# Moving low parts to GpSimd and the list steps closer together at the front of the up stage of a two-layer encoder trunk

## The chip, the cores and the metric

One Trainium2 chip, of which the kernel uses one core. The time is the device time of one execution in microseconds, the median of several runs. The engines are TensorE (PE in the profile; PEld is its weight load), VectorE (DVE), ScalarE (ACT), GpSimd (POOL) and SyncE (SP), each with an instruction queue that it works off in order; transfers run on 16 DMA engines.

## The reference

The trunk has two layers on 256 tokens of width 1024: a latent attention and a sparse attention, each followed by an expert mixer (PEER). The change lies in the mixer, which both layers have. Its core:

```python
best, pos = lax.top_k(cand, PEER_TOPK)                     # per token and head: 16 of 16384 experts
expert = jnp.take_along_axis(cand_idx, pos, axis=-1)
gate = jax.nn.softmax(best, axis=-1)
...
u = w_down[e_blk]
a = jnp.einsum('td,ted->te', x_blk, u).astype(jnp.float32)
hg = (jax.nn.gelu(a, approximate=False) * g_blk).astype(w_up.dtype)
return jnp.einsum('te,ted->td', hg, w_up[e_blk]).astype(x_blk.dtype)
```

There are 8 heads with 16 experts each, so 128 experts per token, out of 128 x 128. Inputs and outputs are float32.

## The kernel before

**Staging.** A layer's mixer computes the queries and the scores, picks experts on VectorE and GpSimd, and then streams the expert tables through TensorE. The *down stage* multiplies all 128 blocks of 128 experts of `w_down` with the 256 tokens and leaves the gated activations in a large array `A` in SBUF (`arena` in the profile). The *up stage* multiplies activations with rows of `w_up` into four PSUM banks `y`. float32 products are made of two float16 parts, high and low: a product is high x high + high x low + low x high, three matmuls for one.

**The stream of weights.** `Stream` (lines 178 to 299) carries every weight block (128 x 1024, float32, 512 KB) from memory. `_load` (210) brings a block into one of six `raw` buffers: by SyncE for a whole block (222), by an indirect DMA of GpSimd for a *listed* one (219). `_high` (233) makes the high part on ScalarE (line 166), `_low` (240) the low part on VectorE (line 175), with a sum that a later check of the number range uses. High and low parts have rings of six. `get` (279) takes the next block and splits up to three blocks ahead and loads up to eight ahead. If `share` is n, every n-th block goes through `_pooled` (246) in `_split` (268): ScalarE scales the raw block in place (253) and rounds it to the high part (255), GpSimd subtracts (257), and four blocks later ScalarE makes the sum (266). Both layers use this in earlier stages, where `share` is 4 or 3; in the up stage it is 0.

**The up stage** (from 1623) has 118 blocks. The first 22 (`HEAD`) are dense: a block of 128 experts for both token tiles, twelve matmuls in `rows` (500). Then come 72 listed blocks with 24 further dense ones in between (two at a time). A listed block holds one expert row per partition, picked so that only experts that some token chose are fetched: 40 of them serve both token tiles, 32 serve one (six matmuls). `USES` holds the order, `PAIRS` and `FIRSTS` say which pairs of activations it needs and from which use on. `cut` (1536) splits a pair of activations into high (`xh`, ScalarE) and low (`xl`, VectorE).

**The lists.** Which rows a listed block holds comes from the chosen experts. `lists` (1398) is a generator of 24 steps, mostly on VectorE: taking the eight largest of a row and replacing them, again and again (1417, 1418), then ranks, one small TensorE product `base` (1441), four one-hot tiles `to` (1480), each with eight small matmuls that send entries to other partitions (`moved`, 1475), and at the end the row numbers `up_at` (1491) and `act_at` (1493, 1496). `list_on(n)` (1513) makes n steps. Two calls of `list_on(3)` come in the last blocks of the down stage, the rest in the head of the up stage.

**Stores and returns.** Activations that listed blocks need are first stored to memory: `store` (1501) issues one transfer of 256 KB on SyncE (1508). `gather` (1519) then returns them by row number, two or three indirect DMAs on GpSimd into a tile `V` or `U` (1527, 1532). The first three gathers are issued in the head, each later one three groups ahead of its use.

**What sets the order.** A planner orders the instructions of each engine, except where the code forces it. `pe` and `dve` (444, 447) put each instruction behind the one before it on TensorE and VectorE, as long as the chain has an entry in `chains`. Both chains are on from the down stage until they are dropped in the head (`chains.pop`). While they are on, rows, list matmuls, lows, activation splits and list steps run in the order in which they are written. ScalarE's, GpSimd's and SyncE's order is the planner's, but `gp` (453) puts a gather behind the last indirect load written ahead of it.

Of the kernel before, what the change touches and what calls it, by code (L numbers as in the profile page):

```python
# [68 lines left out]
DENSE, HEAD = 46, 22  # L69
# [260 lines left out]
def tile_trunk(ctx: ExitStack, tc: tile.TileContext, ins, out: bass.AP, short, shared):  # L330
# [17 lines left out]
    def oh_tile(tag, dt=F32):  # L348
        return ohp.tile([P, 4, P], dt, tag=tag, name=tag)
# [64 lines left out]
    ws = Stream(nc, raws, rings, half, split, spare16)  # L414
# [38 lines left out]
    def gp(emit):  # L453
        with ExitStack() as order:
            if ws.fetched is not None:
                order.enter_context(tc.issue_after(ws.fetched))
            return emit()
# [42 lines left out]
    def rows(o4, lhs, blk, start, stop, tiles=(0, 1)):  # L500

        h, l = blk
        lh, ll = lhs
        for t in tiles:
            tsl = slice(t * P, (t + 1) * P)
            todo = [(w, rr, i, n) for i, (w, rr) in enumerate(((lh, h), (lh, l), (ll, h))) for n in range(2)]
            if stop:
                todo.sort(key=lambda z: z[3])
            for w, rr, i, n in todo:
                ins = mm(o4[t][n], w[:, tsl], rr[:, n * 512 : (n + 1) * 512], start and i == 0, stop and i == 2)  # L510
        return ins
# [663 lines left out]
    def peer(li):  # L1175
# [325 lines left out]
        def store(half, upto):  # L1501

            b0 = stored[half]
            b1 = min(b0 + CHUNKED, NKEYS)
            if b0 < b1 <= upto:
                ts = slice(half * P, (half + 1) * P)
                rows_of = abuf[(b0 - DENSE) * P : (b1 - DENSE) * P, ts].rearrange("(b a) t -> a b t", a=P)
                nc.sync.dma_start(rows_of, A[:, b0:b1, ts])  # L1508
                stored[half] = b1
# [3 lines left out]
        def list_on(n):  # L1513
            for _ in range(n):
                next(listing[0], None)
# [3 lines left out]
        def gather(g):  # L1519
            if g >= len(GROUPS):  # L1520
                return
            t = oh_tile("VU"[g % 2])
            for slot, c in enumerate(GROUPS[g][:2]):
                at = act_at[:, c : c + 1]
                if c < BOTHS:
                    o = t[:, 2 * slot : 2 * slot + 2, :].rearrange("p a b -> p (a b)")
                    gp(lambda: nc.gpsimd.indirect_dma_start(o, None, abuf, bass.IndirectOffsetOnAxis(ap=at, axis=0)))  # L1527
                    continue
                halves = abuf.rearrange("e (h t) -> (e h) t", h=2)
                for h in range(2):  # L1530
                    at = act_at[:, c + h * JO : c + h * JO + 1]
                    gp(lambda: nc.gpsimd.indirect_dma_start(t[:, 2 + h, :], None, halves,  # L1532
                                                            bass.IndirectOffsetOnAxis(ap=at, axis=0)))
            gathered[g] = t

        def cut(n):
            if n >= len(PAIRS):
                return
            kind, k = PAIRS[n]
            if kind == "listed":  # L1540
                a = gathered.pop(k).rearrange("p (s h) t -> p s (h t)", s=2)
            else:
                a = A[:, k : k + 2, :]
            slot = slice(2 * n % NC, 2 * n % NC + 2)
            hh, al = xh[:, slot, :], xl[:, slot, :]
            total = split.total("most")
            act(lambda: split.high(hh, a, A_UNIT))
            dve(lambda: split.low(al, a, A_UNIT, hh, total))
            made[n] = [(hh[:, j, :], al[:, j, :]) for j in range(2)]
# [51 lines left out]
        def operand(k):  # L1601
            if k % 2 == 0 and k not in parts:
                a = A[:, k : k + 2, :]
                slot = slice(k % NC, k % NC + 2)
                hh, al = xh[:, slot, :], xl[:, slot, :]
                total = split.total("most")
                split.high(hh, a, A_UNIT)
                split.low(al, a, A_UNIT, hh, total)
                for j in range(2):
                    parts[k + j] = (hh[:, j, :], al[:, j, :])  # L1610
            return parts[k]
# [3 lines left out]
        def middle_loads():  # L1615
            held.append(load_x(lnar, keep))
            held.append(load_affine(lnar, li, 1))
            if last and short:
                least()
                split.seen = BOTH + split.n["most"]  # L1620
                weigh_up(0, 0, split.seen)

        if short:
            for i, (n, slot, tiles) in enumerate(USES):
                if i == FIRSTS[n]:
                    cut(n + 1)
                    if PAIRS[n][0] == "listed":
                        gather(PAIRS[n][1] + 3)
                if i < len(USES) - STAGGER:
                    rows(y4, made[n][slot], ws.get(), i == 0, False, tiles)  # L1630
                if i < HEAD - 9:
                    list_on(1)
                    store(0, NKEYS)
                    store(1, NKEYS)
                if i == HEAD - 9:
                    list_on(99)
                    while stored != [NKEYS, NKEYS]:
                        store(0, NKEYS)
                        store(1, NKEYS)
                    chains.pop("dve")  # L1640
                    chains.pop("pe")
                if HEAD - 9 <= i < HEAD and (HEAD - 1 - i) % 3 == 2:
                    gather((i - HEAD + 9) // 3)
                if i == len(USES) // 2:
                    middle_loads()
            items = [(made[n][slot], tiles) for n, slot, tiles in USES[-STAGGER:]]
        else:
            for k in range(NKEYS - STAGGER):
                rows(y4, operand(k), ws.get(), k == 0, False)
                if k == 64:  # L1650
                    middle_loads()
            items = [(operand(k), (0, 1)) for k in range(NKEYS - STAGGER, NKEYS)]
# [67 lines left out]

    mla()
    peer(0)
    dsa()
    return peer(1)


# [91 lines left out]
```

## Time and profile before

| | us |
|---|---|
| median of 3 runs (1676.13 to 1681.88) | 1680.58 |
| the profiled execution | 1678.09 |
| its span, first to last instruction | 1676.3 |
| granted TensorE clock | 0.992 |

A row of a timeline gives the start and the length in microseconds, the engine, the line, the operation, what it writes and reads, the number of instructions merged, and in brackets the idle time before it and what ended that. A row of groups gives the busy time and the mean in ns, then the idle time before. A row of waits says who waited for whom: total, times, longest. A line like L460 or L175 is a helper's, so the names of the tiles tell where an instruction belongs: `y` is the up stage, `d` the down stage, `raw<-in_up,up_at` a listed load, `V<-abuf` or `U<-abuf` a return, `lo` a low part of a weight block and `xl` one of an activation pair.

### The profile page before, as it was taken

The numbers are of one execution on the slowest core, as the hardware profiler recorded it, in microseconds if no ns is written. First come the engines' busy times: TensorE is split into PE (matmuls) and PEld (weight loads), VectorE is DVE, ScalarE is ACT, GpSimd is POOL, SyncE is SP. The second block draws the span as 40 slices with busy tenths as digits, with TensorE's granted clock in tenths as the row PEclk, the third lists the DMA queues.
The fourth block names the chain that finished last, engine by engine and source line by source line (L and its number), as shares of the span: only waits on it lengthen the run. The fifth ranks groups of instructions, "written<-read, shape, count | busy, mean of one in ns | idle before, by whom it ended". The sixth has DMA issues, their size and how long they took to land.

```text
span 1676.3 us, 33243 instructions
## 1 busy us (share of the span) xinstructions
PE 1609.7 (96%) x12451; PEld 1163.6 (69%) x12451; DVE 1347.5 (80%) x3212; ACT 1064.2 (63%) x1865; POOL 531.3 (32%) x419
## 2 busy tenths in 40 slices
PE   9999999999999999999899999999999999999995
PEld 7678888999996443444577688888999974444432
DVE  8689999989997756666788799999989978466565
ACT  7666656888884445554568665576888854455452
POOL 2011255000000277877032022441000000788783
PEclk9999999999999999999999999999999999999998
DMA  9445656655758677777855555556547567777773
GB/s 342 157 171 173 203 179 208 209 164 179 231 184 249 243 256 250 265 259 244 298 199 172 185 184 179 202 183 218 169 154 252 181 206 271 247 262 254 271 241 132
DMA packets 139963, 361.44 MB, mean 216 GB/s; under 512 B 13712, under 2 KB 56848, under 8 KB 139792
## 3 DMA queue, kind: packets, MB, share of 16 engines
q1 hardware_dynamic: 112880, 268.51, 47.8%
q0 software_dynamic: 26624, 90.20, 16.5%
q8 instruction: 99, 1.62, 0.4%
q14 instruction: 72, 0.59, 0.1%
q10 hardware_dynamic: 288, 0.52, 0.1%
HBM read 333.35 MB, written 25.82 MB: 214 GB/s over the span
## 4 chain that ended last, share of the span: by engine, by line
PE 51%; DMA 11%; issue 11%; POOL 11%; DVE 11%; ACT 3%; SPq 2%; POOLq 0%; DVEq 0%; ACTq 0%
PE d L460 34%; DMA raw<-in_up,up_at 7%; DVE lo L175 5%; POOL raw L219 5%; PE y L460 4%; PE G L460 3%; PE pq L460 2%; POOL U L1527 2%; POOL U L1532 2%; PE seen L460 2%; ACT hi L166 2%; SPq L1508 1%; DMA raw<-in_up 1%; POOL V L1532 1%; PE qw L460 1%
## 5 line engine op out<-in xcount | busy, mean ns | idle before, releaser
L175 DVE SCALAR_TENSOR_TENSOR lo<-raw,hi 128x1024 f16<-128x1024 f32 (+2 forms) x550 | 695.5, 1275 | 217.0 <-ACT hi L166 169.6
L166 ACT ACTIVATE hi<-raw 128x1024 f16<-128x1024 f32 (+2 forms) x550 | 570.0, 1050 | 384.9 <-DMA raw<-in_up,up_at 169.1
L460 PE MATMUL d<-xh,lo 128*128 128x256 f16 x2048 | 558.5, 273 | 0.9 <-DVE lo L175 0.9
L460 PE MATMUL d<-xh,hi 128*128 128x256 f16 x2048 | 558.6, 273 | 0.0
L460 PE MATMUL d<-xl,hi 128*128 128x256 f16 x2048 | 558.5, 273 | 0.0
L460 PEld LDWEIGHTS <-hi 128*128 128x128 f16 x5016 | 489.0, 98 | 57.7 <-issue 0.9
L219 POOL DMA_INDIRECT raw<-in_up,up_at x144 | 172.1, 1195 | 612.4 <-DVE act_at L1496 566.0
L460 PEld LDWEIGHTS <-xh 128*128 128x128 f16 x1904 | 185.4, 98 | 251.2 <-issue 32.0
L460 PE MATMUL y<-lo,xh 128*128 128x512 f16 x880 | 265.2, 379 | 12.0 <-DVE lo L175 8.1
L460 PE MATMUL y<-hi,xh 128*128 128x512 f16 x880 | 264.0, 380 | 11.3 <-ACT hi L166 5.8
L460 PEld LDWEIGHTS <-lo 128*128 128x128 f16 x2508 | 245.8, 98 | 31.9 <-DVE lo L175 2.7
L460 PE MATMUL y<-hi,xl 128*128 128x512 f16 x880 | 264.4, 380 | 2.1 <-DVE xl L175 1.9
L1375 ACT ACTIVATE gate<-hot,rest 128x128 f16<-128x128 f16 x512 | 168.0, 406 | 20.6 <-DVE hot L1369 18.7
L460 PEld LDWEIGHTS <-xl 128*128 128x128 f16 x952 | 92.1, 98 | 120.9 <-DVE xl L175 7.5
L257 POOL TENSOR_TENSOR lo<-raw,hi 128x1024 f16<-128x1024 f32 x27 | 63.3, 2346 | 212.1 <-ACT hi L255 161.1
L1369 DVE TENSOR_TENSOR hot<-iota,place 128x1024 f16<-128x1024 f16 x128 | 87.7, 689 | 19.3 <-PE G L460 18.6
L460 PE MATMUL G<-gate,hot 128*128 128x128 f16 x1024 | 96.2, 219 | 2.1 <-DVE gate L1371 2.1
L460 PEld LDWEIGHTS <-hot 128*128 128x128 f16 x1536 | 92.8, 113 | 3.1 <-DVE gate L1371 2.4
L1290 POOL TENSOR_TENSOR arena<-arena 128x800 f32<-128x800 f16 x32 | 70.7, 2210 | 62.7 <-DVE arena L1287 62.7
L460 PE MATMUL seen<-gate,hot 128*128 128x128 f16 x512 | 89.1, 219 | 0.0
L1371 DVE TENSOR_TENSOR gate<-hot,gate 128x512 f16<-128x512 f16 x128 | 87.6, 687 | 0.0
L253 ACT ACTIVATE raw<-raw 128x1024 f32<-128x1024 f32 x27 | 28.6, 1057 | 88.7 <-DMA raw<-in_down 80.1
(270 smaller groups left out, 1828.2 us busy)
## 6 DMA issues: line engine op xcount, KB each, us to landing
raw<-in_down SPq DMA_DIRECT2D x256, 512.0 KB
raw<-in_up SPq DMA_DIRECT2D x92, 512.0 KB
abuf<-arena SPq DMA_DIRECT2D x80, 256.0 KB
raw<-in_peer_q SPq DMA_DIRECT2D x24, 512.0 KB
raw<-in_dsa_qk SPq DMA_DIRECT2D x16, 512.0 KB
raw<-in_mla_w_o SPq DMA_DIRECT2D x8, 512.0 KB
arena<-in_peer_q SPq DMA_DIRECT2D x8, 512.0 KB
raw<-in_dsa_v SPq DMA_DIRECT2D x8, 512.0 KB
```

The costliest lines, as they stand in the source:

```text
L166: return nc.scalar.copy(o, src) if unit == 1.0 else nc.scalar.mul(o, src, unit)
L175: return nc.vector.scalar_tensor_tensor(o, src, unit, hi, op0=ALU.mult, op1=ALU.subtract, accum_out=total)
L219: self.fetched = self.nc.gpsimd.indirect_dma_start(t, None, table, bass.IndirectOffsetOnAxis(ap=at, axis=0)).ins
L253: self.act(lambda: nc.scalar.mul(raw, raw, unit))
L257: nc.gpsimd.tensor_tensor(lo, raw, hi if short else hi.bitcast(F32), op=ALU.subtract)
L460: return pe(lambda: nc.tensor.matmul(o, l, r, start=start, stop=stop, skip_group_check=True))
L1290: nc.gpsimd.tensor_tensor(o.rearrange("p k c -> p c k"), same, cell[t][:, h, :, None].to_broadcast([P, CELLS, TOPK]), op=ALU.mult)
L1369: nc.vector.tensor_tensor(hot, iota4[:, None].to_broadcast([P, 2, P, 4]), place16[:, :, None, four].to_broadcast([P, 2, P, 4]), op=ALU.is_ ...
L1371: engine.tensor_tensor(gate[:, 0], hot[:, 1].rearrange("p c j -> p j c"), gate16[:, four, None].to_broadcast([P, 4, P]), op=ALU.mult)
L1375: nc.scalar.mul(gate[:, 1, j, :], hot[:, 1, :, j], rest[:, t : t + 1])
L1527: gp(lambda: nc.gpsimd.indirect_dma_start(o, None, abuf, bass.IndirectOffsetOnAxis(ap=at, axis=0)))
L1532: gp(lambda: nc.gpsimd.indirect_dma_start(t[:, 2 + h, :], None, halves, bass.IndirectOffsetOnAxis(ap=at, axis=0)))
```

## The change

```diff
         if short:
+            ws.share = 3
             for i, (n, slot, tiles) in enumerate(USES):
...
-                if i < HEAD - 9:
-                    list_on(1)
+                if i < HEAD - 12:
+                    list_on(2 if i < 8 else 1)
                     store(0, NKEYS)
                     store(1, NKEYS)
-                if i == HEAD - 9:
+                if i == HEAD - 12:
+                    ws.share = 0
                     list_on(99)
...
-                if HEAD - 9 <= i < HEAD and (HEAD - 1 - i) % 3 == 2:
-                    gather((i - HEAD + 9) // 3)
+                if HEAD - 12 <= i < HEAD - 9:
+                    gather(i - HEAD + 12)
```

`share` is 3 from the start of the up stage until block 10 has been taken. `get` splits three blocks ahead, so this concerns blocks 3 to 13 of the head; by their running numbers in the stream (block 0 is number 167 in the first layer, 466 in the second) blocks 5, 8 and 11 of the first layer and 3, 6, 9 and 12 of the second go through `_pooled`. Two list steps stand behind each of blocks 0 to 7 and one behind blocks 8 and 9, where one stood behind each of blocks 0 to 12 and the rest behind 13. The remaining stores, the end of the lists and the end of both chains stand behind block 10 instead of 13. The first three gathers stand behind blocks 10, 11 and 12 instead of 13, 16 and 19.

## The prediction

> **What bounds the kernel now.** I read the page first (busy shares, the 40 slices), then the busy time of each engine in three stretches: the first layer's up stage up to its first listed block, and both layers' from there to the last block.
>
> ```profile
> PE 1609.7 (96%) x12451; PEld 1163.6 (69%) x12451; DVE 1347.5 (80%) x3212; ACT 1064.2 (63%) x1865; POOL 531.3 (32%) x419
> POOL 2011255000000277877032022441000000788783
> ```
>
> Busy time by stretch (columns: length, then PE, PEld, DVE, ACT and POOL busy with counts, granted clock, DMA share, GB/s):
>
> ```profile
> 523.80:587.71 63.91, 58.65 (x299) 26.48 (x297) 48.49 (x124) 26.48 (x32) 9.44 (x9) 1.00 0.79 278
> 587.71:808.61 220.90, 210.97 (x956) 93.55 (x957) 135.91 (x267) 115.95 (x134) 167.45 (x136) 0.99 0.77 260
> 1436.71:1657.39 220.68, 211.60 (x960) 93.12 (x960) 136.88 (x270) 114.64 (x133) 169.96 (x139) 1.00 0.75 249
> ```
>
> Over the whole span TensorE is busy 96%, so no change of this kind can win much; GpSimd has 32%, which looks like room. The slices correct that: it is idle for long and then near 0.8 twice, in the two listed phases. What TensorE needs there comes from its pace:
>
> ```profile
> 526.22 0.59 PE L460 MATMUL y<-hi,xh 128*128 128x512 f16 x2
> 526.65 0.59 PE L460 MATMUL y<-lo,xh 128*128 128x512 f16 x2
> ```
>
> Two matmuls per 0.431 us, so 2.59 us for a dense block of twelve and 1.29 for a listed one with one token tile. From the first listed block on, an up stage has 64 blocks of twelve and 32 of six, 960 matmuls: 206.9 us. The stretches take 220.9 and 220.7, so 14.0 and 13.8 us are lost in them. Next the waits in the first of them, and GpSimd's issues:
>
> ```profile
> ACT hi L166 <- DMA raw<-in_up,up_at: 76.2, 35, 6.2
> PE y L460 <- ACT hi L166: 3.9, 4, 1.6
> PE y L460 <- DVE lo L175: 3.8, 5, 0.9
> ```
>
> ```profile
> 575.83:798.61 222.78, 212.95 (x968) 94.52 (x966) 134.09 (x263) 114.23 (x132) 176.88 (x144) 0.99 0.76 253
> 1424.72:1647.56 222.84, 212.67 (x969) 94.00 (x967) 134.80 (x265) 114.27 (x133) 178.41 (x145) 1.00 0.77 253
> ```
>
> ```profile
> POOL raw L219 <- issue: 20.1, 66, 0.3
> POOL raw L219 <- DVE lo L175: 2.9, 2, 1.7
> ```
>
> TensorE waits for high and low parts, and those for the rows that GpSimd fetches. GpSimd issues 144 indirect DMAs per layer (72 rows of up, 72 returned activations) in 222.8 us, 1.547 each; nearly all its idle time is 0.3 us between two issues, and only 2.9 us are waits for a buffer. So in the listed phase GpSimd's queue is the bound: 222.8 against TensorE's 206.9. What sets its start:
>
> ```profile
> 575.83 1.24 POOL L219 DMA_INDIRECT raw<-in_up,up_at  x1 [283.11 <-DVE act_at L1496]
> 582.39 1.24 POOL L1532 DMA_INDIRECT V<-abuf,act_at  x1 [0.30 <-issue]
> 587.03 0.63 ACT L166 ACTIVATE xh<-V 128x512 f16<-128x512 f32 x1 [0.58 <-DMA V<-abuf,act_at]
> 587.71 0.61 PE L460 MATMUL y<-hi,xh 128*128 128x512 f16 x2 [2.34 <-ACT xh L166]
> 1436.71 0.60 PE L460 MATMUL y<-hi,xh 128*128 128x512 f16 x2 [2.16 <-ACT xh L166]
> ```
>
> It stood 283 us until VectorE had written the lists. The first return goes out behind fetches, and TensorE stands 2.34 and 2.16 us for it. Together a layer has 16.3 (second: 16.0) us that a GpSimd queue far enough ahead would give back.
>
> **Lists earlier.** Of the 24 list steps six are done in the down stage (two calls of `list_on(3)`). The other 18 stand now at blocks 0 to 12 with the last five behind block 13; then at 0 to 9. VectorE runs lows, return splits and list steps in the written order:
>
> ```profile
> 528.22:575.15 46.93, 44.94 (x237) 20.60 (x236) 42.88 (x111) 20.87 (x24) 0.00 (x0) 1.00 0.81 286
> ```
>
> ```profile
> 528.22 0.69 DVE L1569 TENSOR_TENSOR arena<-arena,d 128x512 f32<-128x512 f32 x1 [2.51 <-ACT d L1568]
> ```
>
> ```profile
> L175 DVE SCALAR_TENSOR_TENSOR lo<-raw,hi 128x1024 f16<-128x1024 f32 x19 | 23.0, 1222 | 3.4 <-ACT hi L166 3.4
> L175 DVE SCALAR_TENSOR_TENSOR xl<-arena,xh 128x512 f16<-128x512 f32 x10 | 6.9, 686 | 0.0
> L1480 DVE TENSOR_TENSOR to<-iota,at 128x1024 f16<-128x1024 f16 x4 | 4.7, 1221 | 0.0
> L1417 DVE MAX8 U<-V 128x8 f32<-128x128 f32 x4 | 1.2, 292 | 0.0
> L1418 DVE MATCH_REPLACE8 V<-U,V 128x128 f32<-128x128 f32 x4 | 1.1, 276 | 0.0
> ```
>
> From 528.22 to the lists' end it idles 3.4 us. 19 lows are 21.8 at 1.15 each (1.222 in the record, but neighbours overlap, as the four `to` show: 4.7 of busy, not 4 x 1.221), ten splits at 0.61 are 6.1, L1569 0.6; the lists are the other 15.0 of the 43.5. With the change only lows 3 to 12 and five splits stand ahead of the lists' end, and lows 5, 8 and 11 go to GpSimd: 7 x 1.15 + 3.0 + 0.6 + 15.0 = 26.7, so 554.9 if VectorE never waits. With what it waits for (next part) I take 560: 15 us earlier. The second layer gives lows 3, 6, 9 and 12 away.
>
> **What GpSimd makes of it.** The seven issues of the first three returns go out at once, 7 x 1.55 = 10.9 us, and the last lands 4.6 us after its issue (582.39 to 587.03): at 575.5, 12 us ahead of use. So 2.34 and 2.16 us are gone. A fetch is tied to buffers: fetch 30 takes raw buffer 24, free after low 24, whose place in the ring of six is free after block 18. That is blocks 19 to 29 ahead of use, nine of 2.59 and two of 1.29, less 2.3 for high and low: 23.6 us. Before:
>
> ```profile
> 597.58 1.41 POOL L219 DMA_INDIRECT raw<-in_up,up_at  x1 [0.31 <-issue]
> 607.54 0.59 PE L460 MATMUL y<-hi,xh 128*128 128x512 f16 x2
> ```
>
> Block 30 begins 10.0 us after its fetch is issued. So the lead can grow by up to 13.6, and over the stage GpSimd falls 222.8 - 206.9 = 15.9 behind: 2.3 us are left as waits. If lows stay only three blocks ahead, as `AHEAD` writes them, the lead is 20.7 and 5.2 are left. If nothing can be banked, all 14 are left. I take 3, since VectorE has little other work after the lists. A fetch that waits for its buffer now holds the returns queued behind it on GpSimd, and through them ScalarE's splits; nobody waits for those while the lead lasts.
>
> **TensorE in front.** Its order is written by hand until the chains are dropped, so a list matmul holds all rows behind it. Before:
>
> ```profile
> 549.73 0.16 PE L1441 MATMUL base<-n,below 128*128 128x1 f16 x1 [1.33 <-DVE n L1435]
> 567.30 0.37 PE L1475 MATMUL moved<-sent,to 128*128 128x32 f16 x8 [0.33 <-DVE to L1480]
> ```
>
> 1.33 and twice 0.33: 2.0 us. In the new order `base` stands behind block 4, which ends at 537.9 (the 526.22 row begins block 0's second tile: + 1.29 + 4 x 2.59). Ahead of it VectorE has 0.6, two splits 1.2, three lows 3.5 and 5.8 of steps (seven takes of a MAX8 and a replacement, about 0.6 each with their starts; the sums and the count, an estimate of 1.5): 11.1, so 539.3, a wait of 1.5. The first send stands behind block 6 (544.5), in the same block as its `to`; VectorE has five lows 5.8, four splits 2.4, 0.6 and 10.6 of steps (15.0 less three `to` and a last step of 1.0), 19.4, so 547.6: a wait of 3.1. The third send adds 0.4. That is 5.0, or 3.0 more than before, if GpSimd disturbs nothing. It does:
>
> ```profile
> L257 POOL TENSOR_TENSOR lo<-raw,hi x27: 2124/2133/3114, 105.0 to 1108.3; 128x1024 f16<-128x1024 f32 x27
> ```
>
> ```profile
> 1106.62 1.21 DVE L175 SCALAR_TENSOR_TENSOR lo<-raw,hi 128x1024 f16<-128x1024 f32 x1
> 1108.93 2.63 DVE L175 SCALAR_TENSOR_TENSOR lo<-raw,hi 128x1024 f16<-128x1024 f32 x1
> ```
>
> ```profile
> 1108.35 2.13 POOL L257 TENSOR_TENSOR lo<-raw,hi 128x1024 f16<-128x1024 f32 x1 [10.85 <-ACT hi L255]
> ```
>
> A VectorE low that meets a GpSimd low ends 1.08 us after it: it was held. The 1.15 us that VectorE saves on a low can thus be paid back with 0 to 2.13: little where one-input MAX8 steps fill the time, all of it at the `to` steps, two-input like a low. A gap of 2.3 us can also slow the clock:
>
> ```profile
> 589.29 1.06 PE L460 MATMUL y<-lo,xh 128*128 128x512 f16 x2
> 590.14 1.91 PE L460 MATMUL y<-hi,xl 128*128 128x512 f16 x4
> ```
>
> Behind the 2.34 us gap about eight matmuls ran at 0.43 instead of 0.216, 1.6 us more; behind the 2.16 of the second layer none did. So the front costs between 2 (the wait for `base` covered; not less, since the first send waits for a `to` of its own block) and 5.0 + 3 x 2.13 + 1.6 - 2.0 = 11 us more than before. I take 5.5, nearer the lower end, since two of the lows meet MAX8 and small steps.
>
> The Trainium skill bears on both rows. "GPSIMD Engine Reference", section 1, says that GpSimd's SBUF interface is shared with VectorE's two-input instructions, and section 4.1 advises VectorE for elementwise work; by that the moved lows buy nothing and the front's upper end holds, which the 2.63 us row supports. "TensorE: Matmul & The Clock Gate", in "Why this matters for your kernels", lets idle gaps of up to about 3 us pass; by it 1.6 us would fall out of the upper end, but the 2.34 us row speaks against it.
>
> **What costs nothing.** ScalarE:
>
> ```profile
> L253 ACT ACTIVATE raw<-raw x27: 1042/1058/1062, 87.0 to 1101.9; 128x1024 f32<-128x1024 f32 x27
> L266 ACT ACTIVATE spare<-lo x27: 1041/1044/1062, 108.8 to 1114.6; 128x1024 f16<-128x1024 f16 x27
> ```
>
> ```profile
> 537.04 1.06 ACT L166 ACTIVATE hi<-raw 128x1024 f16<-128x1024 f32 x1 [6.54 <-DMA raw<-in_up]
> ```
>
> A moved low adds a scaling and a sum pass, about 2.2 us; ScalarE is busy 26.5 of the front's 63.9 and idles for loads. If that cover were gone, a high would come 2.2 later. A moved block's raw buffer is free some 2 us later (one more ScalarE pass, and 2.13 for 1.15); the block that loads into it is used six blocks, 15 us, later. SyncE's stores keep their places in blocks 0 to 9; the others move up three blocks, and they had all been issued soon after:
>
> ```profile
> 534.42 4.46 SPq L1508 DMA_DIRECT2D abuf<-arena  x5
> ```
>
> The last ended at 538.9, with TensorE in block 5: nothing gained or lost. GpSimd's queue in front holds nothing but the moved lows, so nothing waits behind them.
>
> **Sum.** Per layer 16.2 given back, less 3 left over, less 5.5 in front: 7.7; both layers 15.4. The profiled execution took 1678.09 us (span 1676.3, 1.8 around it): 1662.7. It lies 2.5 under the median of the runs, 1680.58, so I forecast a median of 1665.
>
> **Rivals.**
> - *The buffers don't let GpSimd ahead.* Only the first returns gain, 11 of the 14 stay: 16.2 - 11 - 5.5 = -0.3 a layer, about 1681. For it: dense loads by SyncE, which are limited by buffers alone, and the same ring. Against: GpSimd waited for a buffer only twice. Chance 0.16.
> - *GpSimd's lows hold VectorE, and TensorE's written order passes it on (slower).* The front's lows meet the `to` steps: 5.0 + 6.4 and two slow spells of 1.6, 14.6 in all, 12.6 more than before; the fetches start later with it and 7 of the 14 stay: 16.2 - 12.6 - 7 = -3.4 a layer, 1680.58 + 6.8 = 1687. It decides once front and left-over together exceed 18.7 us a layer. For it: the 2.63 us row; against: half the list steps read one input. Chance 0.11. [...]
> - *The lists aren't earlier.* VectorE's work is moved, not removed; if its queue still puts the head's lows first as now (19 in that stretch, up to block 21's, ahead of the lists' end), the start gains 3 us for 5.5 in front: +5, about 1686. Against: the chain now covers the last step. Chance 0.07.
>
> **How the numbers follow.** The forecast has 0.66. Its own range: front 2 and nothing left over, 14.2 a layer, 1652; front 8 and 5.2 left, 3.0, 1674. Two layers behave alike, so errors add. 0.3% is 5 us, about what a measurement here tells from no change: faster is under 1675.5, slower over 1685.6. The first rival's spread puts 0.05 of its 0.16 under 1675.5, 0.10 between; the third is half same, half slower. Faster 0.71, same 0.14, slower 0.15. The range runs from 1652 to 1682.
>
> **What would show it.** Right: act_at written near 560 and 1409; no wait of TensorE at the first listed block; the 144 issues spread over more than 222.8 us with waits for buffers early on; the 960 matmuls in under 212 us; front waits at `base` and the sends of 4 to 11 us. Wrong: a first GpSimd issue after 570, a listed phase still near 220, or front waits over 14 us.

## The result and the profile after

Measured beside each other, four runs each: before 1681.23 us (1676.13 to 1682.76), after 1656.61 us (1650.55 to 1669.58), a ratio of 0.9869 with a 95% interval of 0.9836 to 0.9901. Two later measurements on other chips gave 0.9908 (0.9891 to 0.9925) and 0.9865 (0.9846 to 0.9884). So the change gains 0.9 to 1.4%, some 15 to 23 us. Single executions of the changed kernel lie 20 us apart, and the profiled one below is the longest of its four (1669.58 us, span 1667.7); why is a question of its own.

The page of the changed kernel, TensorE and GpSimd over the span, and GpSimd's 40 slices:

```profile
PE 1609.6 (97%) x12451; PEld 1165.0 (70%) x12451; DVE 1355.1 (81%) x3198; ACT 1079.4 (65%) x1886; POOL 544.0 (33%) x426
...
POOL 3011255000001467877032012441000004678783
```

The two stretches near 0.8 begin one slice earlier than before. By stretch (the columns as in the prediction): block 0 to block 22 and block 22 to block 117 of each layer, then GpSimd's 144 issues of each layer.

```profile
521.60:590.23 68.63, 60.80 (x300) 27.01 (x298) 54.85 (x127) 36.25 (x45) 26.63 (x20) 0.95 0.91 303
590.23:797.39 207.16, 206.23 (x955) 93.32 (x954) 131.82 (x255) 112.56 (x129) 153.85 (x127) 1.00 0.79 261
1366.67:1434.47 67.80, 60.30 (x302) 27.24 (x299) 54.69 (x125) 37.18 (x48) 26.06 (x21) 0.97 0.91 305
1434.47:1648.61 214.14, 208.65 (x956) 93.36 (x955) 133.40 (x260) 111.88 (x128) 161.46 (x129) 0.99 0.74 243
558.79:788.54 229.75, 229.75 (x1066) 104.14 (x1065) 148.59 (x287) 124.31 (x142) 172.68 (x144) 1.00 0.78 257
1402.92:1639.91 236.99, 231.87 (x1064) 104.00 (x1063) 148.86 (x289) 123.68 (x142) 179.67 (x144) 0.99 0.76 251
```

The kernel before, cut at the same blocks (its first front is in the prediction):

```profile
587.71:807.31 219.60, 210.56 (x954) 93.42 (x955) 134.61 (x265) 114.65 (x133) 167.45 (x136) 0.99 0.77 260
1436.71:1656.09 219.38, 210.30 (x954) 92.63 (x955) 136.83 (x270) 114.64 (x133) 168.88 (x137) 1.00 0.76 251
```

The fronts grew from 64 to 68 us at a lower granted clock, the listed phases fell from 219.5 to 207.2 and 214.1. The timeline shows how GpSimd got ahead:

```profile
558.79 2.12 POOL L1527 DMA_INDIRECT V<-abuf,act_at  x1 [7.52 <-DMA arena<-in_ln_gain]
...
585.25 0.94 POOL L219 DMA_INDIRECT raw<-in_up,up_at  x1 [3.38 <-DVE lo L175]
...
590.23 0.59 PE L460 MATMUL y<-hi,xh 128*128 128x512 f16 x2
...
608.36 0.59 PE L460 MATMUL y<-hi,xh 128*128 128x512 f16 x2
```

The first issue goes out at 558.79 instead of 575.83; counted from block 0, which began 2.2 us sooner in this profile, it is 14.8 us earlier. Block 22 (590.23) has no bracket: TensorE waits for nothing there. Fetch 30 is issued 23.1 us ahead of its use (608.36) instead of 10.0. But it stood 3.38 us for a buffer, and GpSimd's waits tell how often that happens now (2.9 us in all before):

```profile
POOL raw L219 <- DVE lo L175: 15.9, 8, 3.4
```

In front, TensorE behind the list matmuls:

```profile
537.92 0.16 PE L1441 MATMUL base<-n,below 128*128 128x1 f16 x1 [1.96 <-DVE n L1435]
...
548.21 0.40 PE L1475 MATMUL moved<-sent,to 128*128 128x32 f16 x8 [4.92 <-DVE to L1480]
548.45 1.01 PE L460 MATMUL y<-hi,xh 128*128 128x512 f16 x2
...
552.67 0.81 PE L460 MATMUL y<-hi,xl 128*128 128x512 f16 x2
```

Pairs of matmuls take 1.01 behind the send's gap instead of 0.59: half speed until about 553. What the moved lows do to VectorE:

```profile
540.27 2.13 POOL L257 TENSOR_TENSOR lo<-raw,hi 128x1024 f16<-128x1024 f32 x1 [9.80 <-ACT hi L255]
...
548.50 2.77 POOL L257 TENSOR_TENSOR lo<-raw,hi 128x1024 f16<-128x1024 f32 x1 [6.10 <-ACT hi L255]
...
540.23 0.18 DVE L1446 TENSOR_SCALAR U<-U 128x32 f32<-128x32 f32 x1
540.45 1.99 DVE L1447 TENSOR_SCALAR U<-U 128x32 f32<-128x32 f32 x1
...
549.21 3.14 DVE L175 SCALAR_TENSOR_TENSOR lo<-raw,hi 128x1024 f16<-128x1024 f32 x1
```

The small operation at 540.45 takes 1.99 us (its neighbour of the same shape, one row up, 0.18) and ends with GpSimd's low at 542.4; the low at 549.21 takes 3.14 instead of 1.22 and ends 1.1 us after GpSimd's.

### The profile page after: what moved, and what is told of

The parts are those of the page before. It is cut to its first block, busy times and chain, and to the rows that moved or that the text cites. A ratio compares the mean times of both kernels' runs of the same rounds, so it can differ in the third digit from the quotient of the medians.

```text
span 1667.7 us, 33248 instructions
## 1 busy us (share of the span) xinstructions
PE 1609.6 (97%) x12451; PEld 1165.0 (70%) x12451; DVE 1355.1 (81%) x3198; ACT 1079.4 (65%) x1886; POOL 544.0 (33%) x426
## 4 chain that ended last, share of the span: by engine, by line
PE 52%; DMA 13%; issue 11%; POOL 11%; DVE 10%; ACT 2%; SPq 1%; POOLq 0%; DVEq 0%; ACTq 0%
PE d L460 34%; DMA raw<-in_up,up_at 7%; POOL raw L219 5%; DVE lo L175 4%; PE G L460 3%; PE y L460 2%; DMA U<-abuf,act_at 2%; PE pq L460 2%; POOL U L1527 2%; PE seen L460 2%; PE q L460 2%; POOL U L1532 1%; DMA V<-abuf,act_at 1%; ACT hi L166 1%; PE v L460 1%
## 5 line engine op out<-in xcount | busy, mean ns | idle before, releaser
L175 DVE SCALAR_TENSOR_TENSOR lo<-raw,hi 128x1024 f16<-128x1024 f32 (+1 forms) x543 | 692.5, 1283 | 192.7 <-ACT hi L166 187.6
L166 ACT ACTIVATE hi<-raw 128x1024 f16<-128x1024 f32 (+1 forms) x543 | 563.7, 1048 | 325.5 <-DMA raw<-in_up,up_at 116.7
L257 POOL TENSOR_TENSOR lo<-raw,hi 128x1024 f16<-128x1024 f32 x34 | 77.5, 2280 | 719.2 <-ACT hi L255 680.5
L253 ACT ACTIVATE raw<-raw 128x1024 f32<-128x1024 f32 x34 | 35.9, 1055 | 95.9 <-DMA raw<-in_down 78.5
```

Of the source, the lines that this page charges most:

```text
L166: return nc.scalar.copy(o, src) if unit == 1.0 else nc.scalar.mul(o, src, unit)
L175: return nc.vector.scalar_tensor_tensor(o, src, unit, hi, op0=ALU.mult, op1=ALU.subtract, accum_out=total)
L253: self.act(lambda: nc.scalar.mul(raw, raw, unit))
L257: nc.gpsimd.tensor_tensor(lo, raw, hi if short else hi.bitcast(F32), op=ALU.subtract)
```

## The experiments

All kernels in one table. Each pair is the first and the second layer, in us from the profile: block 0 to block 22; block 0 to GpSimd's first issue; that issue to the end of the last; block 0 to block 117; then the ratio of the times to the kernel before on the same chip. Behind the first two rows there are three chips: A (again, no_share, late_returns, late_close), B (the next four runs) and C (the last four). A profile shows one execution, and it can lie some us off the median of its kernel.

| kernel | front | first issue | 144 issues | block 0 to 117 | ratio |
|---|---|---|---|---|---|
| before | 63.9, 64.2 | 52.0, 52.3 | 222.8, 222.8 | 283.5, 283.6 | 1 |
| after | 68.6, 67.8 | 37.2, 36.3 | 229.7, 237.0 | 275.8, 281.9 | 0.9869 |
| again (A) | 69.5, 66.8 | 37.9, 35.5 | 236.1, 233.7 | 283.7, 275.7 | 0.9908 |
| no_share (A) | 65.9, 68.1 | 35.7, 36.4 | 236.7, 235.6 | 281.1, 280.2 | 0.9889 |
| late_returns (A) | 69.0, 66.7 | 37.6, 36.2 | 235.7, 230.3 | 282.3, 275.2 | 0.9903 |
| late_close (A) | 70.1, 68.6 | 45.9, 43.4 | 231.5, 230.7 | 287.0, 280.9 | 0.9955 |
| before_again (B) | 64.5, 64.8 | 52.0, 52.2 | 222.7, 224.0 | 284.4, 285.1 | 1.0001 |
| lag_no_share (B) | 64.0, 63.5 | 44.6, 43.9 | 224.6, 225.2 | 278.4, 276.6 | 0.9935 |
| lag_base (B) | 65.0, 64.5 | 42.3, 44.6 | 221.1, 230.3 | 271.9, 283.6 | 0.9893 |
| sends_last (B) | 59.0, 58.9 | 47.2, 46.9 | 222.0, 224.1 | 278.1, 279.7 | 0.9968 |
| fewer_before (C) | 62.8, 61.5 | 52.7, 52.0 | 206.7, 207.0 | 271.4, 272.2 | 0.9783 |
| fewer_after (C) | 68.7, 68.2 | 37.3, 36.5 | 222.7, 222.7 | 274.6, 274.1 | 0.9815 |
| lag_base_2 (C) | 64.6, 64.4 | 41.6, 44.5 | 224.3, 227.2 | 274.4, 277.8 | 0.9888 |
| again_2 (C) | 69.3, 67.1 | 37.8, 35.8 | 229.7, 225.1 | 276.6, 273.1 | 0.9865 |

(In the fewer kernels there are 128 issues.) The theory was that of the forecast: GpSimd's queue bounds the listed phase, and its earlier start is the gain. Block 117 follows the end of the last issue by 6.2 to 9.7 us in every layer except three kernels' (the two fewer kernels, 11.9 to 15.0, and the second layer of again_2, 12.1). So where the queue is the bound, a stage is the first issue, the length of the queue and about 8.5 us.

**The changed kernel again, twice.**

> The changed kernel once more, unchanged. Its profiled execution was the longest of its four (1669.58 against 1650.55 to 1657.20 us), with 2.3 us lost in the listed phase of the first layer but 8.2 in that of the second. If these 8.2 us belong to the change, the new profile shows them again. If they are spread between executions, the second layer's stretch from block 22 to block 117 is near 208 us as in the first, and the profiled time near 1657.

> The changed kernel a third time, beside the other three on one chip. Expected: a ratio to the kernel before between 0.986 and 0.992, as in its two earlier measurements (0.9869 and 0.9908).

Measured 0.9908 (0.9891 to 0.9925) and 0.9865 (0.9846 to 0.9884). Block 22 to block 117 of both layers, first again, then again_2:

```profile
589.80:804.06 214.26, 208.74 (x955) 93.66 (x954) 132.38 (x257) 113.08 (x130) 153.74 (x127) 0.99 0.77 255
1434.07:1642.97 208.90, 206.70 (x955) 93.34 (x954) 133.11 (x258) 111.52 (x128) 157.52 (x127) 1.00 0.74 249
```

```profile
592.44:799.83 207.39, 206.24 (x955) 93.34 (x954) 132.19 (x255) 112.81 (x129) 154.91 (x127) 1.00 0.78 260
1435.79:1641.70 205.91, 205.91 (x956) 93.34 (x955) 134.66 (x260) 113.32 (x131) 151.10 (x129) 1.00 0.76 253
```

The 8.2 us of the first profile's second layer do not belong to that layer: here the first layer of again loses as much and its second 3, and again_2 loses almost nothing (the stretch's 954 matmuls without a wait are 205.9, the last row). They are spread between executions. With the first profile the six layers leave 1.3, 8.2, 8.4, 3.0, 1.5 and 0.0 us, a mean of 3.7.

**The moved lows left out** (`ws.share` stays 0).

```diff
-            ws.share = 3
...
-                    ws.share = 0
```

> The changed kernel without the moved lows: share stays 0, list steps and returns as changed. Theory: a low made by GpSimd holds VectorE's two-input work behind it, so what VectorE saves (three or four lows of 1.15 us a layer) is paid back; without them the lists end within 2 us of 558 and the time is within 4 us of the changed kernel, rather below it. Rival: the moved lows are what lets VectorE finish the lists early; then the first send's wait grows from 4.9 to over 8 us and the kernel is 6 to 9 us slower than the changed one.

Measured 0.9889 (0.9870 to 0.9908), beside 0.9908 for again on the same chip: the same, if anything faster. The first issue comes as early. The send's wait is not longer, as the rival had it, but shorter (timeline, first layer):

```profile
547.91 0.36 PE L1475 MATMUL moved<-sent,to 128*128 128x32 f16 x8 [2.58 <-DVE to L1480]
```

2.58 us here and 4.27 in the second layer, against 4.83 and 4.67 in again. What VectorE saves on three or four lows it pays in held operations. In every layer of the changed kernel's three profiles three operations of VectorE in front, lows and list steps, take 0.7 to 2.0 us longer each than without the moved lows. One is the step at 540.45, whose row in no_share is

```profile
540.80 0.18 DVE L1447 TENSOR_SCALAR U<-U 128x32 f32<-128x32 f32 x1
```

Together the three hold it for 4.3 to 5.4 us a layer, against 3.45 or 4.6 saved (three or four lows at 1.15). The Trainium skill, "GPSIMD Engine Reference", section 4.1, sends elementwise work to VectorE; these runs agree as far as they can tell: a low takes GpSimd 2.13 us and VectorE 1.22.

**The returns late again.**

```diff
-                if HEAD - 12 <= i < HEAD - 9:
-                    gather(i - HEAD + 12)
+                if HEAD - 9 <= i < HEAD and (HEAD - 1 - i) % 3 == 2:
+                    gather((i - HEAD + 9) // 3)
```

> The changed kernel with the first three gathers behind blocks 13, 16 and 19 as before; lists and moved lows as changed. Theory: only the early start of GpSimd's queue counts, and with a lead of 20 us and more nobody waits for a return, whatever stands ahead of it: within 3 us of the changed kernel, no wait at the first listed block. Rival: returns right behind the lists are the gain; then a wait of about 2 us at block 22 comes back in each layer and the kernel is 4 to 5 us slower.

Measured 0.9903 (0.9886 to 0.9921), the same as again, and no wait at block 22: the place of the returns is worth nothing. With no_share this leaves the pace of the list steps, with the earlier close of the lists, as what gains; no run leaves out the moved lows and the early returns together.

**The last list step later, the front the same.**

```diff
-                if i < HEAD - 12:
-                    list_on(2 if i < 8 else 1)
+                if i < HEAD - 9:
+                    if i < 9:
+                        list_on(2 if i < 8 else 1)
...
+                if i == HEAD - 9:
...
-                if HEAD - 12 <= i < HEAD - 9:
-                    gather(i - HEAD + 12)
+                if HEAD - 9 <= i < HEAD - 6:
+                    gather(i - HEAD + 9)
```

> The changed kernel with the last list step, the end of the chains and the gathers three blocks later (behind blocks 13, 14, 15); the other list steps as changed, so TensorE's front is the same. GpSimd's first return goes out about 7 us later, near 565. Theory: the lead is capped by the raw buffers (GpSimd waited 9.2 us for them in its first twelve fetches), so the later start only takes these waits away: within 3 us of the changed kernel, GpSimd's early waits down to 2 to 3 us. Rival: each us that GpSimd starts earlier is a us of lead; then the kernel loses about 7 us a layer, 10 to 14 in all.

Measured 0.9955 (0.9935 to 0.9975): by the ratios (0.9955 - 0.9908) x 1684.3 = 7.9 us above again, by the medians (1677.45 and 1666.97) 10.5. GpSimd's first issue in the timeline:

```profile
570.35 1.58 POOL L219 DMA_INDIRECT raw<-in_up,up_at  x1 [16.69 <-DMA raw<-in_up]
```

GpSimd's waits for buffers in the first layer (total, times, longest), here and then in again:

```profile
POOL raw L219 <- DVE lo L175: 9.5, 4, 4.6
```

```profile
POOL raw L219 <- DVE lo L175: 21.6, 9, 6.1
```

Counted from block 0 the first issue is 8.0 and 7.9 us later, and the stage 3.3 and 5.2 longer. The theory was wrong, and the rival's 10 to 14 us are too much by the ratios and just met by the medians. The waits for buffers fall by half, so about half of a later start is free, and half is paid. The size is rough, since this profile is the longest of its eight executions and that of again one of the shortest of its six.

**TensorE's front cleared of waits.** Three kernels move the list matmuls to later blocks. lag_no_share is no_share with this; lag_base and its repeat add the steps per block named in their expectation; sends_last starts from the kernel before.

In lag_no_share, lag_base and lag_base_2:

```diff
                 yield
-                send()
+                if j0 == 8:
+                    send()
+            send()
+            send()
+            yield
+            send()
             yield
```

In sends_last:

```diff
                 yield
-                send()
+            while sends:
+                send()
             yield
```

> The kernel of no_share with every list send one block later: the first send stands behind block 7 instead of 6, the second and third behind 8, the fourth behind 9, the last step behind 10. In no_share TensorE stood 2.6 and 4.3 us for the first send and ran at half speed behind it. Theory A: TensorE's front and GpSimd's queue bound the stage together, since a fetch waits for a raw buffer that TensorE's progress frees: with the send's wait mostly gone (0 to 2 us) GpSimd's early buffer waits shrink too, and the kernel gains 2 to 4.5 us a layer on no_share, a ratio to the kernel before near 0.985. Rival B: GpSimd's queue alone sets the end, so what TensorE waits in front is free: within 2 us of no_share, a ratio near 0.989.

> As lag_no_share, and the small product base one block later too (steps per block 2, 2, 2, 2, 0, 3, 3, 2, 1, 1): its wait of 1.96 us in no_share should fall to near 0, with the list's end within 1 us of lag_no_share. Theory A: 1 to 2 us a layer faster than lag_no_share, a ratio near 0.983. Rival B: the same as no_share and lag_no_share, near 0.989. If VectorE is the engine that is late, the wait only moves from base to the first send and the time is that of lag_no_share.

> The kernel before with gentler steps (per block 2, 2, 2, 2, 0, 2, 1, 2, 1, 1, 1, 0, 0), all four sends and the last step behind block 13, and the first returns behind blocks 13, 14 and 15; no moved lows. TensorE's front should lose no more than the 2.0 us of the kernel before; GpSimd starts near 566, 8 us later than in the changed kernel. By late_close (a start 12 us later cost 3 to 5 us a layer) the later start costs about 3 us a layer, and the front gives 5 to 6 back. Theory A: 2 to 3 us a layer faster than the changed kernel, a ratio near 0.987. Rival B (only GpSimd's start counts): 3 to 8 us a layer slower than the changed kernel, a ratio near 0.995.

> The kernel of lag_base once more, on the same chip as the changed kernel. In the profiles its front was 65 us against the changed kernel's 67 to 69, and GpSimd started 42 to 45 us after block 0 against 35 to 38. Theory: what the front saves (3 us) and what the later start costs (about a third of 7 us) cancel: within 4 us of again_2. Rival: it is the better version, 5 us or more under again_2.

Measured 0.9935 (0.9920 to 0.9950), 0.9893 (0.9878 to 0.9908), 0.9968 (0.9951 to 0.9985) and 0.9888 (0.9858 to 0.9917). The clearest is sends_last; its front, its listed phase and its 144 issues in the first layer:

```profile
519.91:578.89 58.98, 58.03 (x299) 26.38 (x297) 47.37 (x122) 25.50 (x31) 9.30 (x9) 1.00 0.85 291
578.89:797.96 219.07, 210.21 (x955) 93.42 (x955) 136.01 (x267) 115.61 (x134) 166.88 (x136) 0.99 0.78 263
...
567.15:789.15 222.00, 213.14 (x969) 94.63 (x968) 134.74 (x265) 113.89 (x132) 176.17 (x144) 0.99 0.76 254
```

The front is the shortest of all, with one wait of 0.9 us, 8 to 10 us under the changed kernel's. The listed phase gives all of it back, 219 as before the change: 47.2 to the first issue, 222.0 of queue and 8.8 make 278. By the ratio it gains 5.4 us on the kernel before and is far from the changed one (its profiled execution, 1666.57 us, is 5.5 under the median of its twelve, so the stages in the table look better than the kernel is). GpSimd starts 11.7 us ahead of block 22, hardly other than before the change (11.9), and waits only 3.5 us for buffers in this layer. So theory A's price was wrong here: a wait of TensorE in front is mostly free while GpSimd's start is the bound, and rival B is nearer. Whether it is free in the changed kernel too, where GpSimd waits 14.1 to 21.6 us a layer for buffers that the work on the blocks frees, sends_last does not show. For lag_no_share profile and time disagree: its stages are 3 us shorter than no_share's, its ratio is worse, on another chip. The profile of no_share is the longest of its six executions, and the two medians are equal (1666.11 and 1666.00 us), so the two kernels can't be ranked. lag_base moved its wait, as its last sentence feared: `base` waits no more, the first send does (waits of TensorE in the first layer's front).

```profile
PE moved L1475 <- DVE to L1480: 4.3, 1, 4.3
```

But its time is not that of lag_no_share, as that sentence had it: on the same chip it is 0.42% faster, some 7 us (5.7 by the medians), while the stages of the two profiles are equal in sum (555.5 and 555.0). Why stays open. On one chip lag_base_2 and again_2 cannot be told apart. The waits that are left in front are for VectorE, and no kernel here is shown to beat the changed one.

**Fewer issues on GpSimd.**

```diff
-                halves = abuf.rearrange("e (h t) -> (e h) t", h=2)
-                for h in range(2):
-                    at = act_at[:, c + h * JO : c + h * JO + 1]
-                    gp(lambda: nc.gpsimd.indirect_dma_start(t[:, 2 + h, :], None, halves,
-                                                            bass.IndirectOffsetOnAxis(ap=at, axis=0)))
+                at = act_at[:, GROUPS[g][0] : GROUPS[g][0] + 1]
+                o = t[:, 2:4, :].rearrange("p a b -> p (a b)")
+                gp(lambda: nc.gpsimd.indirect_dma_start(o, None, abuf, bass.IndirectOffsetOnAxis(ap=at, axis=0)))
```

Both kernels fetch other activations for some blocks than the reference asks for, so their results are not to be used: they show what a shorter queue does to the time.

> The kernel before with less work for GpSimd's queue: where a group returns two halves of activations by two indirect DMAs, one DMA of the same size fetches a whole row by another list column instead, so 16 of the 144 issues of a layer are left out (those blocks then multiply other activations than the reference asks for). Nothing else changes. Theory: GpSimd's queue bounds the listed phase; 16 x 1.55 = 24.8 us less of it puts it under TensorE's 206.9, so block 22 to block 117 falls from 219.6 and 219.4 us to 206 to 209 and the kernel gains 11 to 13 us a layer, a ratio near 0.986, with the lists as late as before. Rival: the waits in that phase come from VectorE's or ScalarE's splits and not from the number of issues; then the stretch stays over 217 and the ratio over 0.997.

> The changed kernel with the same 16 issues a layer left out (same change of the computation). Theory: with GpSimd's queue no longer the bound, the earlier lists buy nothing and the longer front (67 to 69 us from block 0 to block 22 against 64 to 65) shows bare: 2 to 5 us a layer slower than fewer_before, a ratio near 0.990. Rival: earlier lists help for a reason besides GpSimd's queue; then it is as fast as fewer_before or faster, 0.986 or less.

Measured 0.9783 (0.9761 to 0.9805) and 0.9815 (0.9798 to 0.9831). Block 22 to block 117, both layers, first of fewer_before, then of fewer_after:

```profile
587.27:795.84 208.57, 206.59 (x955) 93.13 (x954) 137.85 (x273) 116.64 (x135) 156.89 (x121) 1.00 0.83 280
1420.28:1631.04 210.76, 207.57 (x958) 93.96 (x956) 140.25 (x272) 117.65 (x137) 145.92 (x124) 0.99 0.79 265
```

```profile
592.45:798.36 205.91, 205.91 (x956) 93.34 (x955) 138.55 (x264) 116.36 (x131) 136.78 (x112) 1.00 0.82 268
1427.39:1633.29 205.90, 205.90 (x955) 93.38 (x954) 136.57 (x260) 114.32 (x131) 135.34 (x114) 1.00 0.76 253
```

This settles the bound: with the lists as late as before, 16 issues fewer take 11 and 9 us out of the listed phase. And with the queue out of the way the change costs: its listed phase has no wait left, but its front is 6 to 7 us longer, and it is 0.32% slower, 5.4 us (the two intervals just overlap; the stages of the profiles differ by 5.1 us the same way). Both gained more than expected, in part since something behind the stage gains as well (next section).

**The kernel before, a second profile.**

> The kernel before, unchanged, for a second profile of it. Its first profiled execution (1678.09 us) lay 3 to 6 us under the medians measured since, so its losses may be understated. Expected: ratio 1.000 within 0.002; a wait of about 2 us at block 22 in each layer; block 0 to block 117 between 283 and 288 us in each layer (283.5 and 283.6 in the first profile).

Measured 1.0001 (0.9985 to 1.0017); its stages, in the table, are 1 to 1.5 us longer than in the first profile, with waits of 2.97 and 2.72 us at block 22.

## Why the prediction was right, and where its terms were off

The sum gave 1665 from 1680.58, a ratio of 0.9907; measured were 0.9869, 0.9908 and 0.9865. The mechanism holds, by four runs: fewer issues remove the same loss (fewer_before), a later close brings half of it back (late_close), and without the moved lows (no_share) or without the early returns (late_returns) nothing is lost. That the total came so near is in part luck: the stages of the profiles gave 12.7 of the 15.4 us foreseen, and the end of the kernel, which the sum did not have, gave 1.6 more on average of three profiles.

- *Lists earlier by 15 us*: act_at was written by 558.1 against 560 foreseen. Counted from block 0, which began 2.2 us sooner here, that is 36.5 us against 36.2. The ledger without waits (554.9, so 31.1 from block 0) was 5.4 us short.
- *The lead and what is left over*: 23.1 us against 23.6 at block 30, no wait at block 22, and a mean of 3.7 us left against 3. But that mean is taken over layers that lose 0.0 to 8.4, which one sum did not show.
- *The front, +5.5*: the six fronts average 68.2; the two of before are 61.8 without their first-return waits (2.34 and 2.16): +6.4. In the first layer `base` waited 1.96 against 1.5, the first send 4.9 against 3.1 (the operation held at 540.45, 1.8 us, is as large as the difference); the means of the six layers are 1.5 and 4.5. The half-speed spell behind the first layer's send lost 2.3 us more, which stood only in the upper bound.
- *The moved lows*, priced inside the front's bounds: worth nothing, as the forecast read the Trainium skill, "GPSIMD Engine Reference", sections 1 and 4.1. The front's upper end of 11, which it drew from there as well, did not come.
- *The stage as a sum*: 7.7 us a layer foreseen. The six layers average 277.8 against 284.15 for the four of before: 6.3. With the sizes measured above the forecast's own sum gives 16.2 - 3.7 - 6.4 = 6.1, so the front and the left-over, each sized too small, make up the difference. But the terms are not independent of each other. The same 6.3 is the start (15.4 us earlier) less a longer queue (232 on average of six against 223, mostly waits for buffers), and where GpSimd hardly waits for buffers, as in sends_last, what TensorE loses in front drops out of the stage. How much of the front's 6.4 us is free in the changed kernel itself stays open.

What the sum did not have is the end of the kernel. Before, and in again_2, from the last low part's sum to the first addition behind the stage:

```profile
1655.89 0.24 DVE L686 SCALAR_TENSOR_TENSOR junk<-sums 128x77 f16<-128x77 f32 x1
...
1657.17 0.38 PE L460 MATMUL y<-hi,xl 128*128 128x512 f16 x1
...
1657.91 0.19 ACT L707 CAST sound<-fit 1x1 int32<-1x1 f32 x1
...
1662.50 0.69 DVE L538 SCALAR_TENSOR_TENSOR arena<-arena,y 128x512 f32<-128x512 f32 x1 [6.36 <-issue]
```

```profile
1636.99 0.24 DVE L686 SCALAR_TENSOR_TENSOR junk<-sums 128x77 f16<-128x77 f32 x1
...
1639.01 0.19 ACT L707 CAST sound<-fit 1x1 int32<-1x1 f32 x1
...
1642.78 0.38 PE L460 MATMUL y<-hi,xl 128*128 128x512 f16 x1
...
1643.71 0.69 DVE L538 SCALAR_TENSOR_TENSOR arena<-arena,y 128x512 f32<-128x512 f32 x1 [6.47 <-PE y L460]
```

The number check of the weights needs the sum of the last low part; its verdict goes into an integer (L707) on which the program branches. In all fourteen profiles the first addition starts 4.4 to 4.7 us after L707, and the kernel ends 13.8 us after that. In eleven of them L707 comes within 1 us of the last matmul's end, so 3.8 to 5.3 us pass between the last matmul and the addition, and "issue" as the releaser says that nothing in the profile is being waited for. In again_2 and both fewer kernels the lead lasts to the end: the verdict is out some 4 us before the last matmul ends, and nearly all of that time runs beside the matmuls. The profile names a matmul as the releaser there, but the distance from L707 is the same, as in fewer_before:

```profile
1627.84 0.19 ACT L707 CAST sound<-fit 1x1 int32<-1x1 f32 x1
...
1632.34 0.69 DVE L538 SCALAR_TENSOR_TENSOR arena<-arena,y 128x512 f32<-128x512 f32 x1 [6.27 <-PE y L460]
```

So the verdict, not the last matmul, may set the start of the addition there too; no run parts the two. An execution whose lead lasts gains 3 to 5 us more there, and that is part of why they lie so far apart: between again_2 (1659.32 us) and the first profiled execution (1669.58) the two stages differ by 8.0 us, the stretch behind block 117 of the second layer by 3.3 (15.8 against 19.1), all else by -1.0.

Open are two things. Why the queue takes 225 us in one layer and 237 in another of the same program is not settled; the times of single issues and the waits for buffers both vary. And the profiles of the changed kernel put its gain at 14 us (mean 1664.7 against 1678.7 for the two of before), the medians at 17 to 25; the rest is in executions that left no profile.

## What to carry to other kernels

Where an in-order queue is the bound, price a change by when that queue starts and how long it is, and do not charge waits of the other engines ahead of it in full: as long as the queue itself does not wait for buffers, they are overlapped. Starting the queue earlier pays only as far as its buffers let it run ahead: here about half of each us. Before spending effort on an earlier start, count the queue's entries: 16 of 144 issues less were worth more than lists 15 us earlier (in a kernel that fetches other activations than its result needs).

## What the hardware showed unexpectedly

TensorE's half-speed spells are not tied to gaps above some 3 us. In the fourteen profiles' up stages, all 19 gaps of 3.1 us and more ahead of a list matmul or a row were followed by 6 to 12 matmuls at double length (1.2 to 2.5 us lost), but so were 21 of the 37 gaps of 1.57 to 2.97 us (the prediction's 2.34 us row is one of them). The Trainium skill, "TensorE: Matmul & The Clock Gate", "HAM oscillation — how this bites in real kernels", has the rule that gaps up to about 3.4 us pass; here the measurement differs, and the rows decide. And an operation of VectorE with a single tensor input was held by a GpSimd low as well: 1.99 us instead of 0.18 (the row at 540.45; in fewer_after the same operation took 2.05, and in again and again_2 the one of L1445 took 1.94 and 1.90 instead of 0.24).
